# Two-tile sums one per product, the last row splits six steps earlier, and band matrices in four parts

## The chip, the cores and the metric

The program runs on one core of one Trainium2 chip. Its engines are TensorE (PE, with its weight loads as PEld), VectorE (DVE), ScalarE (ACT), GpSimd (POOL) and SyncE (SP); each takes its own queue of instructions in order, and they meet at semaphores. The metric is the device time of one execution in microseconds, less is better. The times are medians of runs; one further execution was recorded by the hardware profiler, and all rows below are from it.

## The reference, cut to what matters

Two layers of a streaming encoder run over 512 prompt rows and 32 sample rows (T = 544 columns in the kernel's layout, feature dimension on the partitions). Layer 0 mixes by stick-breaking attention and a gated linear recurrence, layer 1 by trailing means over windows of 2, 4, 8 and 16 rows. After either mixer comes the same kind of feed-forward block:

```
def swiglu(x, w_gate, w_up, w_down):
    return (jax.nn.silu(x @ w_gate) * (x @ w_up)) @ w_down
x = x + swiglu(rmsnorm(x, norm_ffn[layer]), ffn_gate[layer], ffn_up[layer], ffn_down[layer])
```

D_MODEL is 1024, D_FF is 2816, all of it float32. The pooling of layer 1 is, for each of four groups of 256 channels, the mean over the last `win` rows less the row itself, then a 256x256 map and a scale; the result is added to x. At the end there is one more RMS norm.

## The kernel before

**Precision.** A float32 operand is split into a high part in the fp32r form (ACT copy, line 822) and the low rest (DVE subtraction, line 823), and a product is made of three matmuls: high by high, high by low, low by high. One such split of a weight tile of 128x1024 is what `Supply.split` issues.

**Feed-forward block.** The 22 tiles of 128 hidden features are worked in 11 pairs, `fp` = 0 to 10. The gate and up products of a pair use a seven-product scheme on 2x2 blocks (`strassen`): 7 forms, each for gate and for up, so 14 products `n` = 0 to 13 of 12 matmuls (line 925). The forms of a pair are a11, t1, t2, t3, a12, a22 and t4; t1 and t3 are sums of two weight blocks, and are made by a second DMA that POOL issues with accumulation (line 836) after SP has loaded the first block (line 838); t2 and t4 are added on DVE (line 845).

**Down product.** The product with `ffn_down` is done in groups of hidden tiles, spread over later pairs: `due(fp)` gives the tiles and the half of the 1024 output features that pair `fp` works on. Pairs 1 and 2 work on the group of tiles 0 and 1 (two tiles), pairs 3 to 10 on groups of four, and the last group (18, 19, 21, 20) comes after all pairs: in `last_down` in layer 0, in `final` in layer 1. Each such pair has 8 sums (4 output tiles by 2 halves of the columns); a sum is 3 matmuls per hidden tile into one of the two PSUM banks of the tag `sm` (line 997), then a DVE addition to x (line 1000) that frees the bank. The loop over the products says after which product how many sums are issued: none before product 5, three after it, one after each of 6 to 10.

**Supply.** The order of loads, splits and additions of weights on SP, POOL, ACT and DVE is written out by a planner, the class `Supply`. Every operation has a due step; the clock `beat` ticks once for each product and each sum, and `ahead` issues what has come due, in order, if enough of 17 buffers (`slot`, `give`) are free. If a product needs a weight that has not been split yet, `need` issues the operations up to it at once. `pair` and `rows` hold the due steps. A `ffn_down` row block is a load (SP, line 802) and a split. For the last group the four blocks, in the order (tiles 18 and 19, half 0), (20 and 21, half 0), (18 and 19, half 1), (20 and 21, half 1), have their due steps in one line, counted from step 234, at which the products of the 11 pairs are over:

```
self.rows(PAIRS, ((-9, -5), (-8, -3), (-3, 3), (-1, 5)))
```

The first number of each is the load, the second the split. Layer 1 has a `Supply` of its own; its first loads (t1 and a11 of pair 0) are written after the block of layer 0 and take the next free buffers of the same list.

**Order of the queues.** In the feed-forward blocks PE, DVE, ACT and SP keep the written order. POOL is not in that list: a scheduler orders it. Between the layers (pooling) only PE keeps the written order. So an ACT or DVE instruction that is written in the pooling stage can be queued between instructions of the feed-forward block ahead of it.

**Bands.** The pooling of layer 1 uses banded matrices, `bf`, `bm` and `bl`, that POOL builds from memsets, `affine_select` and subtractions. `bands` is called in `ffn` of layer 0 through the table `mid`, in the written order just ahead of product 4 of pair 1. Their first use is after layer 0, in `pool_out`.

Of the kernel before, what the change touches and what calls it, by code (L numbers as in the profile page):

```python
# [9 lines left out]
F32 = mybir.dt.float32  # L10
# [4 lines left out]
P = 128  # L15
# [12 lines left out]
WINDOWS = (2, 4, 8, 16)  # L28
# [3 lines left out]
def kernel(  # L32
# [8 lines left out]
    ve, ac, gp, pe = nc.vector, nc.scalar, nc.gpsimd, nc.tensor  # L41

    cst = ctx.enter_context(tc.tile_pool(name="cst", bufs=1))
    big = ctx.enter_context(tc.tile_pool(name="big", bufs=1))
# [26 lines left out]
    def small(t="sm"):  # L71
        return psm.tile([P, 512], F32, tag=t, name=nm(t))
# [18 lines left out]
    def phase(table):  # L91
        ins = ac.preload_act_table_set(table).ins
        for p in phases[1]:
            tc.add_manual_dep(ins, p.name, nosync, reason="table")
        phases[0], phases[1] = [ins], []
# [111 lines left out]
    class Norm:  # L207
        def __init__(self, gcol):
            self.gcol = gcol
            self.xh, self.xl = [], []  # L210
            self.acc = s2.tile([P, T + NS], F32, tag="nacc", name=nm("nacc"), bufs=1)[:, :T]
# [468 lines left out]
    n1 = []  # L680
# [65 lines left out]
    PAIRS = DFF // P // 2  # L746
# [26 lines left out]
    class Supply:  # L773
# [4 lines left out]
        def __init__(self, l):  # L778
            self.l, self.raw, self.w, self.start = l, {}, {}, None
            self.ops = []  # L780
            for fp in range(PAIRS):
                self.base = 22 * fp - 8 * bool(fp)
                self.pair(fp)
            self.base += 22
            self.rows(PAIRS, ((-9, -5), (-8, -3), (-3, 3), (-1, 5)))
            self.ops.sort(key=lambda o: o[0])

        def due(self, fp):
# [94 lines left out]
    supply = Supply(0)  # L883
# [15 lines left out]
    def one(n):  # L899
        return pone.tile([P, 512], F32, tag="one", name=nm(n))  # L900
# [80 lines left out]
    def ffn(sup, nin, after=None, mid={}, last=None, first=None):  # L981
        hid = {} if first is None else first

        def down(fp):

            fs, hs = sup.due(fp)

            def bank(m, hf, s):
                beat.tick(sup)
                while any(f not in hid for f in fs):  # L990
                    beat.tick(sup)
                c = slice(P * (m % 4), P * (m % 4 + 1))
                ps = small()[:, :HN]
                for i, f in enumerate(fs):
                    (wh, wl), (a, b) = sup.row(f, m // 4), hid[f]
                    for j, (lt, r) in enumerate(((wh, a), (wh, b), (wl, a))):
                        pe.matmul(ps, lhsT=lt[:, c], rhs=r[:, s], start=i == 0 and j == 0,  # L997
                                  stop=i == len(fs) - 1 and j == 2)
                xs = x[:, m, s]
                ve.tensor_add(xs, xs, ps)  # L1000
                if hf and m % 4 == 3:
                    for f in fs[::2]:
                        sup.done((f // 2, m // 4))

            return [lambda a=(m, hf, s): bank(*a) for h in hs for m in range(4 * h, 4 * h + 4) for hf, s in HALVES] if fs else []

        def last_down():


            fs, _ = sup.due(PAIRS)  # L1010
            groups = [(0, 1)] + [(m,) for m in range(2, KD)]
            for ms in groups:
                ps = {(m, h): one("ps")[:, :HN] for m in ms for h in range(2)}
                for i, f in enumerate(fs):
                    for (m, h), o in ps.items():
                        (wh, wl), (a, b) = sup.row(f, m // 4), hid[f]
                        c, s = slice(P * (m % 4), P * (m % 4 + 1)), HALVES[h][1]
                        for j, (lt, r) in enumerate(((wh, a), (wh, b), (wl, a))):
                            pe.matmul(o, lhsT=lt[:, c], rhs=r[:, s], start=i == 0 and j == 0,  # L1019
                                      stop=i == len(fs) - 1 and j == 2, skip_group_check=True)  # L1020
                    if i % 2 or len(ms) > 1:
                        beat.tick(sup)
                for (m, h), o in ps.items():
                    xs = x[:, m, HALVES[h][1]]
                    ve.tensor_add(xs, xs, o)
                for m in ms:
                    beat.later(1, lambda m=m: after(m))
            beat.flush()
            for h in range(2):
                for f in fs[::2]:  # L1030
                    sup.done((f // 2, h))

        for fp in range(PAIRS):
            if fp or first is None:
                prods, sums = strassen(sup, nin, fp, hid), down(fp)
                for n, f in enumerate(prods):
                    if (fp, n) in mid:
                        mid[fp, n]()
                    f()
                    for _ in range(0 if n < 5 else 3 if n == 5 else 1):  # L1040
                        if sums:
                            sums.pop(0)()
        if last:
            last()
        beat.flush()
        if after:
            last_down()
        return hid
# [5 lines left out]
    BW = HN - NS - P  # L1054
    NL = 512 - P - 3 * BW
# [5 lines left out]
    def band(o, win, off):  # L1061

        n = o.shape[1]
        gp.affine_select(o, o, pattern=[[1, n]], compare_op=ALU.is_ge, fill=0.0, base=off, channel_multiplier=-1)
        gp.affine_select(o, o, pattern=[[-1, n]], compare_op=ALU.is_ge, fill=0.0, base=win - 1 - off, channel_multiplier=1)

    def bands():
        eye = big.tile([P, P], F32, name="eye")[:, :BW]
        gp.memset(eye, 1.0)
        band(eye, 1, 15)  # L1070
        eyl = cst.tile([P, NL], F32, name="eyl")[: NL + 15]
        gp.memset(eyl, 1.0)
        band(eyl, 1, 15)
        for g, win in enumerate(WINDOWS):
            gp.memset(bf[:, g], 1.0 / win)
            gp.memset(bm[:, g], 1.0 / win)
            for c in range(win - 1):
                gp.memset(bf[:, g, c : c + 1], 1.0 / (c + 1))
            band(bf[:, g], win, 0)
            band(bm[:, g], win, 15)  # L1080
            gp.tensor_sub(bf[:, g], bf[:, g], ident)
            gp.tensor_sub(bm[:, g], bm[:, g], eye)
            sa = bl[0:NS, g, NL:]
            gp.memset(sa, 1.0 / win)
            band(sa, win, 0)
            gp.tensor_sub(sa, sa, ident[:NS, :NS])
            ha = bl[32:47, g, NL:]
            gp.memset(ha, 1.0 / win)
            band(ha, win, 15)
            la = bl[: NL + 15, g, :NL]  # L1090
            gp.memset(la, 1.0 / win)
            band(la, win, 15)
            gp.tensor_sub(la, la, eyl)
# [16 lines left out]
    def pool_hist(i):  # L1110
        pw, hraw = pool["w"], pool["hraw"]
        if not i:
            ph = small()
            pe.transpose(ph[:, :120], hraw[:120, :P], ident[:120, :120])
            ve.tensor_copy(hist, ph[:, :120].rearrange("p (t k) -> p k t", k=KD))
            ptb.append(slot("pts"))
        phh = small()
        for k in range(4 * i, 4 * i + 4):
            pe.matmul(phh[32:47, 256 * (k // 2 % 2) : 256 * (k // 2 % 2 + 1)], lhsT=hist[:, k],
                      rhs=pw[k // 2][:, 256 * (k % 2) : 256 * (k % 2 + 1)], start=k % 2 == 0, stop=k % 2 == 1)  # L1120
        ac.activation(ptb[0][32:47, 512 * i : 512 * (i + 1)], phh[32:47], AF.Copy)
# [18 lines left out]
    def scales(n):  # L1140
        n.out = n.rs()
        phase("silu_and_others")
# [1 line left out]
    ET = mybir.EngineType  # L1144
    queues = {ET.PE, ET.DVE, ET.Activation, ET.SP}
    with tc.manual_schedule(engines=queues):
        ffn(supply, n1[0], after0, {(0, 3): lambda: scales(n1[0]), (0, 7): lambda: n1[0].out(), (1, 4): bands,
                                    (PAIRS - 1, 7): pool_load}, lambda: [pool_hist(i) for i in range(2)])


# [12 lines left out]
    supply = Supply(1)  # L1163
# [152 lines left out]
    with tc.manual_schedule(engines=queues):  # L1316
        final(supply, ffn(supply, n3, first=first))
# [37 lines left out]
```

## Time and profile before

| what | value |
|---|---|
| runs | 1100.87, 1104.32, 1105.19 us; median 1104.32 |
| profiled execution | 1103.79 us |
| its span, first to last instruction | 1102.0 us |
| mean granted TensorE clock | 0.98 |
| busy: PE, PEld, DVE, ACT, POOL | 95%, 91%, 70%, 45%, 19% of the span |
| chain that ended last, by engine | PE 75%, DVE 10%, issue 6%, ACT 5%, DMA 2%, POOL 1% |
| feed-forward of layer 0, of layer 1 (products and sums) | 267.5 to 655 us, 688 to 1060 us |

The span runs from the first to the last instruction; the profiled execution's time is 1.8 us longer. "Busy" is the share of the span in which an engine works. The chain is the work that ended last, followed back from the end: at each step to what released an instruction, or to the instruction ahead of it on its engine. PE is busy nearly all the time, so what counts is where PE waits, and for whom.

### The profile page before, as it was taken

What the parts mean: (1) busy time and instruction counts of PE and PEld (TensorE: products, weight loads), DVE (VectorE), ACT (ScalarE), POOL (GpSimd) and SP (SyncE); (2) the same over time, 40 slices, a digit from 0 to 9 for tenths busy, and PEclk for the clock granted to TensorE, in tenths of its full rate; (3) what the DMA queues carried; (4) which work ended last, traced back from release to release, by engine and by line L of the source; (5) the groups of instructions that cost most, each with busy time, mean ns of one, the idle gap of its engine ahead of it and who ended that gap; (6) DMA issues with size and microseconds to landing.
All of it is one profiled execution on the core that took longest, in us unless ns stands there. A gap on an engine that the chain in (4) does not pass through costs nothing.

```text
span 1102.0 us, 19760 instructions
## 1 busy us (share of the span) xinstructions
PE 1044.4 (95%) x7971; PEld 1002.9 (91%) x7971; DVE 768.4 (70%) x1236; ACT 491.7 (45%) x825; POOL 210.7 (19%) x331
## 2 busy tenths in 40 slices
PE   8979999999899999999999989599999999999987
PEld 7978888899899999999999878499999999999976
DVE  6776666767777777767776575957777766677643
ACT  7555555544643344332444354644434434334422
POOL 5162225103421101111110211111011111010100
PEclk8989999999999999999999998889999999999999
DMA  8412222414877467756566532256655676656602
GB/s 221 140 50 68 68 58 90 106 52 106 158 158 144 106 120 168 173 135 132 125 127 153 128 88 34 62 116 148 139 116 122 146 172 149 135 122 125 167 33 81
DMA packets 210955, 130.63 MB, mean 119 GB/s; under 512 B 7224, under 2 KB 195872, under 8 KB 210865
## 3 DMA queue, kind: packets, MB, share of 16 engines
q1 hardware_dynamic: 162528, 103.11, 33.2%
q0 software_dynamic: 47696, 25.16, 17.6%
q8 instruction: 62, 1.02, 0.4%
q10 hardware_dynamic: 640, 1.12, 0.3%
q14 instruction: 29, 0.23, 0.1%
HBM read 124.76 MB, written 4.60 MB: 117 GB/s over the span
## 4 chain that ended last, share of the span: by engine, by line
PE 75%; DVE 10%; issue 6%; ACT 5%; DMA 2%; POOL 1%; SPq 0%; ACTq 0%; DVEq 0%; POOLq 0%
PE xy L925 30%; PE sm L997 17%; PE z L925 11%; PE acc L168 10%; ACT ha L822 2%; DVE la L823 2%; DVE sB L474 1%; DMA raw<-in_hyb_w_in_dram 1%; PE ps L1019 1%; PE pa L1173 1%; POOL sA L493 1%; ACT y L1294 1%; DVE y L1300 1%; DMA rt<-in_ffn_up_dram 1%; DVE lt L823 1%
## 5 line engine op out<-in xcount | busy, mean ns | idle before, releaser
L997 PE MATMUL sm<-hh,h 128*128 128x272 f32 x576 | 168.0, 292 | 7.0 <-DVE x L1000 6.2
L836 POOL DMA_DIRECT2D rt<-in_ffn_gate_dram x44 | 57.0, 1295 | 589.4 <-DMA rt<-in_ffn_gate_dram 382.3
L997 PE MATMUL sm<-hl,h 128*128 128x272 f32 x576 | 165.6, 287 | 0.0
L997 PE MATMUL sm<-hh,l 128*128 128x272 f32 x576 | 165.4, 287 | 0.0
L823 DVE TENSOR_TENSOR lt<-rt,ht 128x1024 fp32r<-128x1024 f32 x88 | 107.9, 1226 | 50.7 <-ACT ht L822 50.6
L997 PEld LDWEIGHTS sm<-hh,h 128*128 128x128 f32 x576 | 108.4, 188 | 11.3 <-DVE x L1000 11.3
L98 ACT ACTIVATE s<-s 128x544 f32<-128x544 f32 x44 | 29.0, 659 | 187.1 <-DVE s L934 182.4
L997 PEld LDWEIGHTS sm<-hh,l 128*128 128x128 f32 x576 | 108.4, 188 | 0.0
L997 PEld LDWEIGHTS sm<-hl,h 128*128 128x128 f32 x576 | 108.4, 188 | 0.0
L925 PE MATMUL xy<-b,ha 128*128 128x272 f32 x704 | 103.6, 289 | 0.8 <-DVE x L678 0.8
L823 DVE TENSOR_TENSOR la<-ra,ha 128x1024 fp32r<-128x1024 f32 x66 | 81.0, 1227 | 29.1 <-ACT ha L822 29.1
L822 ACT ACTIVATE ht<-rt 128x1024 fp32r<-128x1024 f32 x88 | 92.5, 1051 | 11.5 <-DVE rt L845 6.1
L925 PEld LDWEIGHTS xy<-b,ha 128*128 128x128 f32 x704 | 93.9, 188 | 1.3 <-DVE x L678 1.0
L1000 DVE TENSOR_TENSOR x<-x,sm 128x272 f32<-128x272 f32 x160 | 69.2, 432 | 31.8 <-PE sm L997 30.8
L168 PE MATMUL acc<-xh,whi 128*128 128x272 f32 x320 | 75.4, 317 | 2.5 <-ACT xh L98 2.5
L836 POOL DMA_DIRECT2D rt<-in_ffn_up_dram x44 | 76.5, 1739 | 2.0 <-DMA rt<-in_ffn_up_dram 1.5
L976 ACT ACTIVATE hh<-u 128x544 fp32r<-128x544 f32 x44 | 29.0, 659 | 97.5 <-DVE u L965 49.9
L822 ACT ACTIVATE ha<-ra 128x1024 fp32r<-128x1024 f32 x66 | 67.3, 1051 | 6.1 <-DMA ra<-in_ffn_up_dram 4.9
L168 PE MATMUL acc<-xl,whi 128*128 128x272 f32 x320 | 68.2, 294 | 0.5 <-DVE xl L228 0.5
L168 PE MATMUL acc<-xh,wlo 128*128 128x272 f32 x320 | 67.9, 293 | 0.0
L925 PE MATMUL xy<-n,ht 128*128 128x272 f32 x352 | 54.1, 295 | 11.4 <-DVE n L293 6.9
L943 ACT ACTIVATE c<-xy 128x272 f32<-128x272 f32 x44 | 17.5, 398 | 95.2 <-PE xy L925 95.2
(381 smaller groups left out, 2525.1 us busy)
## 6 DMA issues: line engine op xcount, KB each, us to landing
r<-in_ffn_down_dram SPq DMA_DIRECT2D x44, 512.0 KB, 6.0
ra<-in_ffn_gate_dram SPq DMA_DIRECT2D x66, 256.0 KB, 5.3
ra<-in_ffn_up_dram SPq DMA_DIRECT2D x66, 256.0 KB, 6.8
rt<-in_ffn_gate_dram SPq DMA_DIRECT2D x44, 256.0 KB, 3.3
rt<-in_ffn_up_dram SPq DMA_DIRECT2D x44, 256.0 KB, 4.5
rt<-in_ffn_gate_dram POOLq DMA_DIRECT2D x44, 256.0 KB, 6.0
rt<-in_ffn_up_dram POOLq DMA_DIRECT2D x44, 256.0 KB, 7.1
raw<-in_hyb_w_in_dram SPq DMA_DIRECT2D x20, 512.0 KB, 3.9
```

Source lines behind the costliest of these rows:

```text
L98: i = ac.activation(*a, **k).ins
L168: pe.matmul(ps[:, h, : s.stop - s.start], lhsT=a[:, wi, :], rhs=b[:, s], start=first and j == 0, stop=last and j == 2)
L474: ve.tensor_tensor_scan(r, r, r, 1.0, op0=ALU.mult, op1=ALU.min)
L493: gp.affine_select(t[:, N - P :], t[:, N - P :], pattern=[[-1, P]], compare_op=ALU.is_gt, fill=fill, base=0, channel_multiplier=1)
L822: ac.activation(hi, raw, AF.Copy)
L823: ve.tensor_tensor(lo, raw, hi.bitcast(F32), op=ALU.subtract)
L836: gp.dma_start(v(t)[:, u], w, accum_op=ALU.add)
L925: pe.matmul(o, lhsT=lt, rhs=r, start=first and n == 0, stop=n == 11, skip_group_check=True)
L943: ac.activation(pc, o, AF.Copy)
L976: beat.later(n, lambda: ac.activation(a, t, AF.Copy))
L997: pe.matmul(ps, lhsT=lt[:, c], rhs=r[:, s], start=i == 0 and j == 0, stop=i == len(fs) - 1 and j == 2)
L1000: ve.tensor_add(xs, xs, ps)
```

## The change

It has three parts.

- **Sums.** In a pair whose group has fewer than four tiles (pairs 1 and 2 of either layer), one sum is issued after each product from product 4 on, until the 8 are done (after product 11). Before, three came after product 5 and one after each of 6 to 10. Pairs with four-tile groups keep their order.
- **Row splits.** The loads and splits of the four row blocks of the last group get due steps 219, 220, 222, 223 (loads) and 225, 226, 228, 230 (splits); before they were 225, 226, 231, 233 and 229, 231, 237, 239. This holds for both layers.
- **Bands.** `bands` is called four times, for one window each, ahead of product 4 of pairs 2, 4, 6 and 8 of layer 0, in place of once ahead of product 4 of pair 1. The two helper tiles `eye` and `eyl` are declared outside of it, and filled in the first call.

```
-            self.rows(PAIRS, ((-9, -5), (-8, -3), (-3, 3), (-1, 5)))
+            self.rows(PAIRS, ((-15, -9), (-14, -8), (-12, -6), (-11, -4)))
...
                     f()
-                    for _ in range(0 if n < 5 else 3 if n == 5 else 1):
+                    few = len(sup.due(fp)[0]) < 4
+                    for _ in range(n > 3 if few else 0 if n < 5 else 3 if n == 5 else 1):
                         if sums:
                             sums.pop(0)()
...
-    def bands():
-        eye = big.tile([P, P], F32, name="eye")[:, :BW]
-        gp.memset(eye, 1.0)
-        band(eye, 1, 15)
-        eyl = cst.tile([P, NL], F32, name="eyl")[: NL + 15]
-        gp.memset(eyl, 1.0)
-        band(eyl, 1, 15)
-        for g, win in enumerate(WINDOWS):
+    eye = big.tile([P, P], F32, name="eye")[:, :BW]
+    eyl = cst.tile([P, NL], F32, name="eyl")[: NL + 15]
+
+    def bands(*gs):
+        if 0 in gs:
+            gp.memset(eye, 1.0)
+            band(eye, 1, 15)
+            gp.memset(eyl, 1.0)
+            band(eyl, 1, 15)
+        for g in gs:
+            win = WINDOWS[g]
...
-        ffn(supply, n1[0], after0, {(0, 3): lambda: scales(n1[0]), (0, 7): lambda: n1[0].out(), (1, 4): bands,
+        ffn(supply, n1[0], after0, {(0, 3): lambda: scales(n1[0]), (0, 7): lambda: n1[0].out(), **{(2 * g + 2, 4): lambda g=g: bands(g) for g in range(4)},
                                     (PAIRS - 1, 7): pool_load}, lambda: [pool_hist(i) for i in range(2)])
```

## Rows read from the trace of the kernel before

**Rows 1.** Windows, layer 0: pair 1, pair 3; span, then busy time of each engine.
```profile
296.54:325.44 28.90, 27.36 (x218) 27.14 (x217) 22.55 (x35) 12.60 (x19) 5.19 (x4) 1.00 0.85 173
...
354.49:387.89 33.40, 33.37 (x266) 33.15 (x266) 23.93 (x36) 13.34 (x20) 5.19 (x4) 1.00 0.61 136
```

**Rows 2.** Waits of PE, whole span: us in total, times, longest.
```profile
PE sm L997 <- DVE x L1000: 6.2, 4, 1.6
...
PE sm L243 <- DVE nacc L219: 4.5, 1, 4.5
...
PE ps L1019 <- DVE x L1025: 2.9, 2, 2.1
PE sm L1285 <- ACT h L822: 2.7, 1, 2.7
...
PE xy L925 <- ACT b L941: 2.1, 1, 2.1
...
PE xy L925 <- ACT a L939: 1.1, 1, 1.1
...
PE sm L1285 <- DVE l L823: 0.6, 1, 0.6
```

**Rows 3.** Timeline of PE in pair 1, layer 0: start, us, instruction, idle before.
```profile
304.06 1.17 PE L925 MATMUL xy<-n,ht 128*128 128x272 f32 x8
...
306.94 0.29 PE L997 MATMUL sm<-hh,l 128*128 128x272 f32 x1
308.77 0.39 PE L997 MATMUL sm<-hh,h 128*128 128x272 f32 x1 [1.54 <-DVE x L1000]
```

**Rows 4.** Timeline of DVE in the same pair.
```profile
303.00 1.22 DVE L823 TENSOR_TENSOR l<-r,h 128x1024 fp32r<-128x1024 f32 x1
...
307.15 1.22 DVE L823 TENSOR_TENSOR la<-ra,ha 128x1024 fp32r<-128x1024 f32 x1 [1.79 <-ACT ha L822]
308.29 0.43 DVE L1000 TENSOR_TENSOR x<-x,sm 128x272 f32<-128x272 f32 x1
```

**Rows 5.** Timeline of ACT from the last product to the end.
```profile
1063.29 1.28 ACT L92 ACT_TABLE_LOAD   x1
1064.58 2.00 ACT L822 ACTIVATE h<-r 128x1024 fp32r<-128x1024 f32 x2
1079.63 0.59 ACT L1294 ACTIVATE y<-sm 32x512 f32<-32x512 f32 x1 [13.04 <-PE sm L1285]
```

**Rows 6.** Timelines of SP, ACT, DVE and PE at the end of layer 0.
```profile
621.76 0.37 SPq L838 DMA_DIRECT2D rt<-in_ffn_gate_dram  x1
...
630.39 0.37 SPq L838 DMA_DIRECT2D ra<-in_ffn_gate_dram  x1
...
635.00 1.06 ACT L822 ACTIVATE ha<-ra 128x1024 fp32r<-128x1024 f32 x1 [4.94 <-DMA ra<-in_ffn_up_dram]
635.96 0.73 ACT L227 ACTIVATE xs<-x,cols 128x544 fp32r<-128x544 f32 x1
...
631.97 1.56 DVE L1025 TENSOR_TENSOR x<-x,ps 128x272 f32<-128x272 f32 x4 [0.47 <-PE ps L1019]
...
639.95 1.22 DVE L823 TENSOR_TENSOR la<-ra,ha 128x1024 fp32r<-128x1024 f32 x1
...
663.19 0.98 PE L243 MATMUL sm<-ones,nacc 128*128 128x1 f32 x4 [4.48 <-DVE nacc L219]
```

**Rows 7.** Window behind that wait; the number after POOL's is the granted clock.
```profile
663.20:668.00 4.80, 4.80 (x25) 4.75 (x26) 2.13 (x8) 2.31 (x6) 0.86 (x2) 0.50 0.93 117
```

**Rows 8.** POOL: one form of line 1064, and its timeline.
```profile
L1064 POOL TENSOR_SCALAR_AFFINE_SELECT eye<-eye x1: 516/516/516, 15.3 to 15.3; 128x112 f32<-128x112 f32 x1
...
214.74 0.61 POOL L1104 DMA_DIRECT2D hraw<-in_state_pool_dram  x1 [5.03 <-issue]
266.80 0.21 POOL L1075 MEMSET bf<- 128x128 f32 x1 [51.45 <-PE acc L168]
...
271.09 1.30 POOL L836 DMA_DIRECT2D rt<-in_ffn_gate_dram  x1
```

## The prediction

> **What bounds the kernel now.** I read the share of busy time first: PE works 95% of the span, so only time in which PE waits, or runs at the lower clock, can be won. The table by stage shows where. A pair with four-tile sums is full: 33.37 of 33.40 us [rows 1]. Pair 1, with two-tile sums, is not: 27.36 of 28.90 us. It issues 14 x 12 + 8 x 6 = 216 matmuls; at 27.36 us / 218 = 0.1255 us each, these want 27.11 us, so 1.79 us are lost. The list of PE's waits names the place: four waits of up to 1.6 us on the addition of line 1000, 6.2 us in all [rows 2], one for each two-tile group in either layer. In the timeline, the second sum's last matmul starts at 306.94 and the third sum's first at 308.77 [rows 3]: 1.83 us where 0.13 us would do. DVE shows why: the first sum's bank is freed by an addition that starts at 308.29, queued behind a weight split begun at 307.15, which had itself waited for ACT [rows 4]. Three short sums in a row want a third bank where there are two.
>
> The same list has two more places that the change touches: the end of the program (line 1285, 2.7 + 0.6 us) and the passage from layer 0 to the pooling (lines 1019 and 243, 2.9 + 4.5 us) [rows 2].
>
> **Part 1, the sums.** Matmuls, evictions, loads and splits keep their number; only their order moves. Now a product lies between two sums, so a bank is wanted again after product, sum, product: 1.51 + 0.75 + 1.51 = 3.8 us (12, 6 and 12 matmuls of 0.1255 us). Ahead of the eviction DVE has at most the split of one form and one addition, 1.22 us each by [rows 4], 2.4 us. So the wait goes and nothing takes its place. The first sum comes a product earlier, at 304.06 [rows 3]; its row weights' low part is ready at 303.00 + 1.22 = 304.22 [rows 4], and is used by the third matmul, at 304.31: just in time. Per group the gain lies between the wait (6.2 / 4 = 1.55 us) and the whole gap (1.83 us); I take 1.75 us, near the 1.79 us by counting, since a restarted PE also loses a little behind the wait. Four groups: **7.0 us**, bounds 6.2 and 7.3.
>
> **Part 2 at the end of layer 1.** I followed the planner's list step by step, with its 17 buffers. Before, the blocks of half 1 are due at steps 237 and 239, but the products end at 234, so `final` has to force both splits through `need`. They then stand on ACT behind the table load at 1063.29 and start at 1064.58 [rows 5]; PE waits 2.7 us for the high and 0.6 us for the low part [rows 2]. With the new steps all four splits lie in pair 10, and no operation finds too few buffers. Both waits go: 3.3 us, and the restart with them; I take **3.4 us**, bounds 2.7 (the low part still late) and 3.6. All of it reaches the end, because the output stage starts on ACT when PE lets it, after 13.04 us idle [rows 5], and its tail hangs on that.
>
> What the splits meet in pair 10: two more of them there, 2 x 1.22 us on DVE and 2 x 1.0 us on ACT (two take 2.00 us [rows 5]). DVE has 9.5 us idle in such a pair, ACT 20 [rows 1], so I cost this at nothing; without that cover it would be 2.4 us a layer. On SP the four row loads move up past nothing but each other; behind them on that queue are only the first loads of the next layer, and behind those, on POOL, their accumulating loads, which can only come earlier.
>
> **Part 2 at the end of layer 0.** Here the half 1 blocks are not late for PE. But layer 1's first loads take over their buffers. Before, the t1 load of layer 1 goes into a buffer that product 13 frees (issued at 621.76), and the a11 load into the raw buffer of a row block, free only once that block's late split is done (630.39) [rows 6]. Now t1 gets a buffer that product 11 frees, and a11 one that product 13 frees: it starts some 8.6 us earlier. Before, ACT meets the split of a11 with its data still on the way and stands 4.94 us, until 635.00, with the norm's copies of line 227 queued behind; the first of these runs at 635.96 [rows 6]. It could have run when the first two of the four additions that start at 631.97 were over, at about 632.75: 3.2 us late. From there DVE and ACT hand each other the work tile by tile to the norm, for which PE waits 4.5 us at 663.19 [rows 2, 6], so a shift of this chain arrives. Three more DVE instructions for layer 1, of 1.2 us each, the first at 639.95 [rows 6], stand inside this chain; with the loads earlier some can go in front of it. I take 3.2 + 1.2 = **4.4 us**; the bounds are 0 (other early splits stand in ACT's way the same) and 3.2 + 3.6 = 6.8. I choose above the middle because a11's wait has a plain cause that is taken away.
>
> After the wait at 663.19, PE runs 4.8 us at a granted clock of 0.50, the lower level of 1.2 GHz [rows 7]. If PE stood less before that, the clock could stay up and those 4.8 us fall to 2.4. The Trainium skill (TensorE: Matmul & The Clock Gate, "HAM oscillation — how this bites in real kernels") says that idle gaps throttle the engine and that it then starts cold; the row agrees, and by that rule the sum would hold up to 2.4 us more. I leave it out of the sum: a shift of 4.4 us mostly moves both ends of this wait.
>
> **Part 3, the bands.** Where the call is written does not place the work: POOL isn't among the queues in written order. `eye`, written in pair 1, is cut at 15.3 us; the load of line 1104, written in pair 10, runs at 214.74; and the first memset of `bf` sits at POOL's head from then to 266.80, until the mixer's last matmuls free its memory [rows 8]. All of that is earlier than the old or the new call, and the four calls' instructions are free to run at the same moment. So I expect the bands where they are, and **0 us**. Bounds: if they did leave, the accumulating load at 271.09 [rows 8] would no longer wait for them, and PE's waits on the copies of lines 939 and 941 in pair 0, 1.1 + 2.1 us [rows 2], could go: 3.2 us. A loss from bands in later pairs has the same size at most, for POOL's pair is otherwise 5.2 of 33 us busy [rows 1].
>
> **Sum.** 1103.79 - 7.0 - 3.4 - 4.4 = 1088.99, so **1089.0 us**. The profiled execution is 0.5 us under the median of the runs, 1104.32, which I neglect.
>
> **The rivals.**
> - *The passage gives nothing.* The scheduler puts another split of layer 1 in front of the norm's copies, and ACT waits for that. For it: the ACT order there comes from a schedule, not from the text, and the old order already misjudged a load. Against: the load comes 8.6 us earlier. 1103.79 - 10.4 = 1093.4 us.
> - *The bands leave as well.* 1089.0 - 3.2 = 1085.8 us. Against it stand the rows of POOL.
> - *The clock stays up.* 1089.0 - 2.4 = 1086.6 us.
> - *The first sum waits instead of the third.* The low row weights come just in time in pair 1 [rows 3, 4]; if every group waits 1.75 us at its first sum, part 1 nets nothing: 1103.79 - 7.8 = 1096.0 us.
> - *DVE becomes the bound in the two-tile pairs, and the kernel slower.* DVE keeps its 22.55 us [rows 1] in a pair that shrinks to 27.1 us, 83%. If evictions came late at each of the 32 sums, it would decide: slower by over 0.5% needs 1103.79 + 5.5, so the 7.8 us of part 2 and 5.5 more have to be lost, 13.3 us over 32 sums, 0.42 us at each, say 1112 us at 0.5. Against it: a bank is free for 3.8 us, and it takes four instructions of 1.22 us in front of an eviction to use that up; the planner puts two there.
> - *The change doesn't do what it says*, of part 3 alone, is in the forecast.
>
> **How the numbers follow.** Chances: the forecast 0.60, the passage gives nothing 0.18, bands 0.07, clock 0.06, first sum 0.05, slower 0.04. A change of 0.5%, 5.5 us, is about what a measurement of this kernel can tell from none: the bound for faster is 1098.8 us. The first five lie below it; for their sizes being smaller together than their bounds, and for runs that spread over 4 us, I take 0.08 of them as no change. Faster 0.88, same 0.08, slower 0.04. Range: the lower end has all upper bounds, 7.3 + 3.6 + 6.8 and the clock's 2.4, 20.1 us: 1084. The upper end has the lower bounds, 6.2 + 2.7 + 0, 8.9 us: 1094.9, and half the spread of the runs, 2.2 us: 1097.
>
> **What would show it.** Right: no wait of line 997 above 0.5 us, pairs 1 and 2 at 27.1 us in both layers; no wait of line 1285 on line 822, and no split behind the table load at the end; the a11 load issued together with that of t1, line 227 first at 1 us after the additions, the wait before line 243 over some 4 us earlier in its stage; bands in one piece behind the mixer's end. Wrong: a wait of line 997 on the row weights, an ACT wait on a load of layer 1 in front of line 227, or band work at the later pairs.

## The result, and the profile after

The changed kernel takes **1089.18 us** (median; 1087.01 to 1090.10) where the kernel before took 1104.51 us beside it: a ratio of 0.9866, 95% interval 0.9844 to 0.9888, or 14.8 us (12.4 to 17.2). Predicted were 1089.0 us. Its profiled execution has a span of 1087.7 us, 14.3 us less. In the changed file the lines behind the loop over the products have moved down by one, those behind `bands` by four.

Where the 14.3 us lie, as differences between the starts of PE's instructions in the two timelines:

| stretch | before, us | after, us | difference |
|---|---|---|---|
| start to the first product of layer 0 | 267.50 | 266.78 | -0.72 |
| pair 0, layer 0 | 29.04 | 29.03 | 0 |
| pairs 1 and 2, layer 0 | 57.79 | 54.23 | -3.56 |
| pairs 3 to 10, layer 0 | 267.24 | 267.25 | 0 |
| history (its transposition to the first sum of the last group) | 5.21 | 7.87 | **+2.66** |
| last group and the wait, to line 243 | 36.41 | 32.53 | **-3.88** |
| line 243 to the first product of layer 1 | 25.08 | 25.59 | +0.51 |
| pair 0, layer 1 | 46.43 | 44.00 | **-2.43** |
| pairs 1 and 2, layer 1 | 57.86 | 54.19 | -3.67 |
| pairs 3 to 10 of layer 1 and the output, to the last matmul | 303.00 | 299.79 | -3.21 |

So part 1 gave 7.2 us, the end of layer 1 gave 3.2, and the passage between the layers 3.1 (2.66 - 3.88 + 0.51 - 2.43). The 0.7 us at the start are no effect of the change: over the profiles of this study that start lies anywhere from 265.1 to 267.8 us. The stretch from line 243 to the first product of layer 1 takes 24.9 to 26.4 us in the twelve profiles in which its first wait is left as it is, so its 0.51 us say little either.

The windows of after, against [rows 1, 7]. Columns: span, busy time of PE, PEld, DVE, ACT and POOL, granted clock, DMA share, GB/s. The stretches are pair 1, pair 3, the history's products and the work behind line 243:

```profile
295.81:322.97 27.16, 27.16 (x219) 27.14 (x217) 22.83 (x36) 12.74 (x19) 5.19 (x4) 1.00 0.89 183
350.04:383.44 33.40, 33.35 (x266) 33.13 (x265) 23.65 (x36) 13.33 (x20) 5.19 (x4) 1.00 0.56 123
619.91:625.16 5.25, 5.25 (x17) 1.88 (x17) 1.22 (x2) 1.65 (x2) 0.83 (x1) 0.67 0.87 105
657.70:662.50 4.80, 4.80 (x28) 4.75 (x29) 2.15 (x8) 2.88 (x7) 1.22 (x3) 0.56 1.06 132
```

Pair 1 is as full as pair 3 now. The third line is new: the history's products ran at a granted clock of 0.67, where they had 1.00 before. The same stretch before:

```profile
623.23:626.78 3.55, 3.55 (x16) 1.45 (x16) 1.21 (x2) 0.59 (x1) 1.53 (x2) 1.00 0.46 136
```

The list of PE's waits, against [rows 2]:

```profile
PE sm L243 <- DVE nacc L219: 4.0, 1, 4.0
...
PE sm L1123 <- DVE hist L1119: 2.4, 1, 2.4
...
PE sm L1289 <- DVE hl L973: 0.4, 1, 0.4
```

The waits of line 997, of line 1019 and of line 1285 on the splits (6.2, 2.9 and 3.3 us) are gone; the wait for the copy of the history was 1.4 us and is 2.4.

Timelines of PE and DVE in pair 1, against [rows 3, 4]: start, length, instruction.

```profile
303.34 0.29 PE L997 MATMUL sm<-hh,h 128*128 128x272 f32 x1
...
303.59 0.36 PE L997 MATMUL sm<-hh,l 128*128 128x272 f32 x1
...
304.16 1.17 PE L925 MATMUL xy<-n,ht 128*128 128x272 f32 x8
...
305.66 0.29 PE L997 MATMUL sm<-hh,h 128*128 128x272 f32 x1
...
303.42 1.22 DVE L823 TENSOR_TENSOR lt<-rt,ht 128x1024 fp32r<-128x1024 f32 x1
304.56 0.43 DVE L1000 TENSOR_TENSOR x<-x,sm 128x272 f32<-128x272 f32 x1
```

The first sum's bank is freed at 304.99, and the third sum doesn't want it before 307.92. The third matmul, the first to use the row weights' low part, shows 0.36 us in place of 0.29: that is all that is left of the rival in which the first sum waits.

The end of layer 0, against [rows 6]: SP, ACT, DVE, PE.

```profile
614.46 0.37 SPq L838 DMA_DIRECT2D rt<-in_ffn_gate_dram  x1
...
616.98 0.37 SPq L838 DMA_DIRECT2D ra<-in_ffn_gate_dram  x1
...
612.87 1.04 ACT L822 ACTIVATE h<-r 128x1024 fp32r<-128x1024 f32 x1
...
620.78 1.06 ACT L822 ACTIVATE ha<-ra 128x1024 fp32r<-128x1024 f32 x1 [0.92 <-DMA ra<-in_ffn_up_dram]
...
631.21 0.75 ACT L227 ACTIVATE xs<-x,cols 128x544 fp32r<-128x544 f32 x1 [4.67 <-DVE x L1025]
...
613.94 1.23 DVE L823 TENSOR_TENSOR l<-r,h 128x1024 fp32r<-128x1024 f32 x1 [1.68 <-ACT h L822]
615.09 0.43 DVE L1000 TENSOR_TENSOR x<-x,sm 128x272 f32<-128x272 f32 x1
...
619.59 0.27 DVE L1119 COPY hist<-sm 128x120 f32<-128x120 f32 x1
...
630.36 1.56 DVE L1025 TENSOR_TENSOR x<-x,ps 128x272 f32<-128x272 f32 x4 [3.06 <-PE ps L1019]
...
657.69 1.76 PE L243 MATMUL sm<-ones,nacc 128*128 128x1 f32 x12 [4.00 <-DVE nacc L219]
```

The a11 load now follows the t1 load by 2.5 us, ACT stands 0.92 us for its data and not 4.94, and line 227 starts 0.85 us behind the start of the additions. New is the line at 613.94: the last of the four row splits stands on DVE for 1.68 us, waiting for ACT, with the addition of line 1000 and the chain to the copy of the history queued behind it.

The end of layer 1 on ACT, against [rows 5], has no split behind the table load; POOL, against [rows 8], has the bands where they were, from the first memset of `bf` to the last subtraction, behind the mixer and in one piece:

```profile
1053.07 1.28 ACT L92 ACT_TABLE_LOAD   x1
1065.40 0.59 ACT L1298 ACTIVATE y<-sm 32x512 f32<-32x512 f32 x1 [11.04 <-PE sm L1289]
...
266.08 0.21 POOL L1079 MEMSET bf<- 128x128 f32 x1 [50.95 <-PE acc L168]
...
285.00 1.44 POOL L1085 TENSOR_TENSOR bf<-bf,ident 128x128 f32<-128x128 f32 x1
```

### The profile page after: what moved, and what is told of

The parts are those of the page before. It is cut to its first block, busy times and chain, and to the rows that moved or that the text cites. A ratio compares the mean times of both kernels' runs of the same rounds, so it can differ in the third digit from the quotient of the medians.

```text
span 1087.7 us, 19757 instructions
## 1 busy us (share of the span) xinstructions
PE 1043.3 (96%) x7971; PEld 1002.0 (92%) x7971; DVE 767.3 (71%) x1236; ACT 492.2 (45%) x825; POOL 210.8 (19%) x331
## 4 chain that ended last, share of the span: by engine, by line
PE 77%; DVE 10%; issue 5%; ACT 3%; DMA 2%; POOL 2%; SPq 0%; ACTq 0%; DVEq 0%; POOLq 0%
PE xy L925 30%; PE sm L997 18%; PE z L925 11%; PE acc L168 10%; PE ps L1019 2%; DVE sB L474 1%; DVE la L823 1%; DMA rt<-in_ffn_up_dram 1%; DMA raw<-in_hyb_w_in_dram 1%; PE pa L1177 1%; ACT ha L822 1%; POOL sA L493 1%; PE pb L1177 1%; DVE y L1304 1%; ACT y L1298 1%
## 5 line engine op out<-in xcount | busy, mean ns | idle before, releaser
L823 DVE TENSOR_TENSOR la<-ra,ha 128x1024 fp32r<-128x1024 f32 x66 | 80.9, 1226 | 24.9 <-ACT ha L822 24.2
L925 PE MATMUL xy<-n,ht 128*128 128x272 f32 x352 | 54.4, 296 | 10.2 <-DVE n L293 7.2
L168 PEld LDWEIGHTS acc<-xh,whi 128*128 128x128 f32 x320 | 50.4, 193 | 9.8 <-issue 5.7
```

What stands on the lines that cost most here:

```text
L168: pe.matmul(ps[:, h, : s.stop - s.start], lhsT=a[:, wi, :], rhs=b[:, s], start=first and j == 0, stop=last and j == 2)
L823: ve.tensor_tensor(lo, raw, hi.bitcast(F32), op=ALU.subtract)
L925: pe.matmul(o, lhsT=lt, rhs=r, start=first and n == 0, stop=n == 11, skip_group_check=True)
```

## The experiments

Ratios are against the kernel before on the same chip; its medians there were 1103.51, 1102.24 and 1104.75 us for the three sets of four.

**Each part alone: the sums.**

```
+                    few = len(sup.due(fp)[0]) < 4
+                    for _ in range(n > 3 if few else 0 if n < 5 else 3 if n == 5 else 1):
```

> The kernel before with part 1 alone (two-tile sums one per product). Theory (a third short sum in a row waits for a bank that DVE frees late): in the two profiled executions pairs 1 and 2 went from 28.9 to 27.1 us in both layers, 7.2 us in all, so 1104.5 - 7.2 = 1097.3 us; no wait of line 997 on line 1000 in the list of waits, and the ends of both layers as before (waits of line 1019 2.9 us, of line 1285 2.7 us). Rival (the sums now wait on their row weights, or the gain is given back at the end of the layer): under 4 us, 1100.5 us or more, with a wait of line 997 on line 822 or 823, or longer waits at lines 1019 and 243.

1097.48 us, ratio 0.994 (0.9923 to 0.9958): 6.6 us (4.6 to 8.5). The four short pairs take 27.17, 27.07, 27.07 and 27.11 us, no wait of line 997 is listed, and the waits at both ends stay. The theory holds. One line of its windows was not expected, in the output stage behind the 2.7 us wait:

```profile
1059.00:1066.00 7.00, 7.00 (x28) 5.03 (x27) 0.51 (x1) 0.00 (x0) 0.00 (x0) 0.70 0.01 2
```

The granted clock is 0.70 behind the wait on the late split; in the profile of before it stayed at 1.00 behind the same wait:

```profile
1065.69:1072.69 7.00, 6.39 (x31) 4.46 (x32) 2.34 (x2) 0.90 (x1) 0.00 (x0) 1.00 0.01 2
```

From pair 3 of layer 1 to the last matmul this kernel needs 305.17 us, before 303.00.

**The row splits alone, in both layers.**

```
-            self.rows(PAIRS, ((-9, -5), (-8, -3), (-3, 3), (-1, 5)))
+            self.rows(PAIRS, ((-15, -9), (-14, -8), (-12, -6), (-11, -4)))
```

> The kernel before with part 2 alone (row loads and splits of the last group six steps earlier in both layers). Theory from the two traces: 3.1 us at the end of layer 0 and 3.1 us at the end of layer 1, 6.2 us, so 1098.3 us, with the four waits of line 997 on line 1000 still there (6.2 us). The prediction's sizes, 4.4 + 3.4 = 7.8 us, would give 1096.7 us. Rival (the passage from layer 0 to the pooling gives nothing of itself): 3.1 us, 1101.4 us.

1097.25 us, ratio 0.9931 (0.9905 to 0.9958): 7.6 us (4.6 to 10.5). The interval holds both sizes, 6.2 and 7.8, and not the rival's 3.1. Its history waits 2.3 us as in the changed kernel, but the clock did not fall behind it:

```profile
623.19:626.74 3.55, 3.55 (x16) 1.45 (x16) 1.22 (x2) 1.64 (x2) 0.85 (x1) 1.00 1.15 144
```

From the history's transposition to the first sum of the last group it takes 6.16 us: 0.95 more than before, all of it the wait.

**The bands alone**, the diff's third part on the kernel before.

> The kernel before with part 3 alone (the band matrices called in four parts in pairs 2, 4, 6 and 8). Theory (POOL takes no notice of where the call is written): no change, 1104.5 us within 0.2%, with the first memset of bf still at 266 us and the last band instruction at about 285 us. Rival (the bands do move): the accumulating load at 271.09 us comes earlier and PE's waits of line 925 on the copies of lines 939 and 941 (1.1 + 2.1 us) go, down to 1101.3 us; or up to 3.2 us more if later pairs' accumulating loads come late.

1102.54 us, ratio 0.9989 (0.9971 to 1.0007): nothing that can be told from no change. The first memset of `bf` starts at 266.15 us, the accumulating load at 270.44. The theory holds.

**The row splits in layer 0 alone, and in layer 1 alone** (the new steps with `if l == 0`, or `if l == 1`, else the old ones).

> The kernel before with part 2 in layer 0 alone. Theory from the traces: the additions and the norm's copies come earlier (3.4 us less between the first sum of the last group and the last, 0.5 us less before line 243), 2.7 us are lost ahead of them, because the extra split in pair 10 delays the copy of the history (wait of the history's products 2.4 us in place of 1.4) and PE's clock then falls (history's products 5.2 us in place of 3.6), and the clock's return in pair 0 of layer 1 decides over 2.4 us: 0.7 us faster without it, 3.1 us with it, so 1101.4 to 1103.8 us. The prediction's step, a shift of 4.4 us that arrives whole: 1100.1 us. Rival (nothing): 1104.5 us.

1100.16 us, ratio 0.9971 (0.9954 to 0.9988): 3.2 us (1.3 to 5.1). From the first sum of the last group to line 243 it takes 32.52 us against 36.41 before, the history 7.85 us against 5.21, and its products 5.24 us, as in the changed kernel. Nothing gained is excluded; the interval holds the first theory's 3.1 and the prediction's 4.4, but not that theory's lower end, 0.7.

> The kernel before with part 2 in layer 1 alone. Theory: the two waits of line 1285 on the late splits (2.7 + 0.2 to 0.6 us) go, which gives 3.2 us, and PE's clock, which fell behind that wait in three of four profiles that have it (0.70 to 0.77 of full speed over some 9 us, 2.2 us lost) and not in the profile of before, stays up: 3.2 to 5.4 us, 1098.1 to 1100.3 us against 1103.5 us. The prediction's size: 3.4 us, 1100.1 us. Rival (the extra splits in pair 10 cost as much as they save): over 1102 us, with waits of PE in pair 10 of layer 1.

1099.65 us, ratio 0.9979 (0.9967 to 0.999): 2.3 us (1.1 to 3.6). From pair 3 to the last matmul its profile has 299.85 us against 303.00, 3.2 us less, and neither wait is left. The 5.4 us are excluded. This suggests that over the runs of the kernel before the clock's fall costs little of its 2.2 us, though three other profiles with that wait (sums, bands and layer 0 alone, 305.1 to 305.3 us) show it whole; only one profile of each kernel is there to see it.

**What delays the history.** The changed kernel with the last row split of layer 0 due at step 231, not 230; on DVE, up to the copy of the history, this only puts the split behind two instructions that stood behind it. On ACT the split of a11 now stands behind the history's two copies from PSUM; both kernels run it after the copy of line 1119.

```
+            self.rows(PAIRS, ((-15, -9), (-14, -8), (-12, -6), (-11, -4 if l else -3)))
```

> The changed kernel with the last of the four row splits of layer 0 due one step later (231 in place of 230), which puts its DVE subtraction behind the addition of line 1000 and the product of line 936, and the split of a11 behind the two copies of the history. Theory (that split delays DVE's chain to the copy of the history by 1.0 us): the wait of PE for the history goes from 2.4 us back to 1.4 us, the history's products take 3.6 us as before, everything behind stays: 1 to 2.7 us faster than the changed kernel's 1089.2 us, 1086.5 to 1088.2 us. Rival (the copy is late because the additions and products of the last products came later, not for the split): the wait stays 2.4 us, 1089.2 us.

The profile shows the theory's mechanism: the copy of the history follows the last product by 1.0 us less, the wait is 1.4 us again, and the products take 3.55 us at a granted clock of 1.00. Its timeline of DVE, and its window of the history's products:

```profile
613.00 0.44 DVE L1000 TENSOR_TENSOR x<-x,sm 128x272 f32<-128x272 f32 x1 [0.70 <-PE sm L997]
613.35 0.72 DVE L936 TENSOR_TENSOR s<-s,rs 128x544 f32<-128x544 f32 x1
613.99 1.22 DVE L823 TENSOR_TENSOR l<-r,h 128x1024 fp32r<-128x1024 f32 x1
...
618.65 0.28 DVE L1119 COPY hist<-sm 128x120 f32<-128x120 f32 x1
```
```profile
618.98:622.53 3.55, 3.55 (x16) 1.45 (x16) 1.21 (x2) 0.59 (x1) 1.82 (x2) 1.00 1.04 178
```

The time, 1087.23 us at 0.9869 (0.9854 to 0.9884), can't be told from the changed kernel's 0.9866. Of the 2.7 us won at the history the profile shows 2.6 lost again in pair 0 of layer 1, which takes 46.58 us here and 44.00 there.

**The history's transposition earlier.**

```
+    def pool_turn():
+        ph = small()
+        pe.transpose(ph[:, :120], pool["hraw"][:120, :P], ident[:120, :120])
+        ve.tensor_copy(hist, ph[:, :120].rearrange("p (t k) -> p k t", k=KD))
...
+    (PAIRS - 1, 12): pool_turn
```

> The changed kernel with the transposition of the history and its copy to SBUF written ahead of product 12 of pair 10 in layer 0 instead of behind product 13. Theory (PE waits there for nothing but this copy): the wait of 2.4 us goes, and the clock that fell behind it in two of three profiles with a wait of 2.3 to 2.4 us stays up (1.7 us): 2.4 to 4.1 us faster than the changed kernel's 1089.2 us, 1085.1 to 1086.8 us, unless the clock takes up to 2.4 us back in pair 0 of layer 1. Rival (the passage is bound by the chain of DVE and ACT and not by PE): the wait before line 243 grows by as much, 1089.2 us.

From pair 10 to the first sum of the last group it needs 37.17 us, the changed kernel 41.28: 4.1 us less, the upper end. The history's products follow the last product at once and take 3.62 us. The wait before line 243 stays (4.1 us), so the rival falls. The time is 1086.43 us, 0.9863 (0.9842 to 0.9883), which can't be told from the changed kernel's; pair 0 of layer 1 again is a long one, 46.72 us, and gives 2.7 us back.

**The bands really moved.**

```
-            gp.memset(bf[:, g], 1.0 / win)
-            gp.memset(bm[:, g], 1.0 / win)
+            ve.memset(bf[:, g], 1.0 / win)
+            ve.memset(bm[:, g], 1.0 / win)
```

> The changed kernel with the two full-size memsets of each window's bf and bm done by DVE, which keeps the written order, so that POOL's band work for bf and bm is really done in pairs 2, 4, 6 and 8 (eight memsets change engine, some 0.2 us each on DVE). Theory (the prediction's bound): the accumulating load at 270.38 us in the trace of the changed kernel no longer stands behind band work and starts by up to 4 us earlier; PE's waits of line 925 on lines 939 and 941 in pair 0 of layer 0 (1.1 + 2.1 us) shrink or go: 0 to 3.2 us faster than 1089.2 us, 1086.0 to 1089.2 us. Rival A (those waits hang on ACT's own queue, with two table loads of 1.28 us in it, and not on the load): 1089.2 us. Rival B (the band work then delays the accumulating loads of pairs 3, 5, 7 and 9): up to 3.2 us slower, with waits of PE on DMA or on line 822 there.

Pair 0 of layer 0 takes 26.27 us in place of 29.03. Its timelines of POOL and PE; its window of pair 0; the same window of the changed kernel:

```profile
252.01 1.28 POOL L836 DMA_DIRECT2D rt<-in_ffn_gate_dram  x1 [38.69 <-DVE tmp L314]
...
278.21 1.27 PE L925 MATMUL xy<-t,ht 128*128 128x272 f32 x8 [2.31 <-ACT b L941]
```
```profile
265.08:291.35 26.27, 23.84 (x184) 23.04 (x184) 20.04 (x32) 16.22 (x28) 2.59 (x2) 1.00 0.47 124
```
```profile
266.78:295.81 29.03, 25.61 (x183) 24.37 (x184) 22.56 (x33) 16.71 (x29) 22.27 (x60) 0.94 0.76 155
```

The band work is now in the later pairs (its first instruction at 326.15 us, in pair 2). The accumulating load starts 18 us earlier, not 4 (16.7 us counted from the first product of layer 0): a memset at POOL's head that waited for the mixer's memory had held it, and then 4.3 us of band work. The wait of line 925 on line 939 (1.1 us) is gone; the one on line 941 is not (2.31 us), so there rival A is right. The rest of the 2.8 us is the clock, 1.00 in place of 0.94 over the pair (29.03 x 0.06 = 1.7 us), and it isn't shown to come from the bands. In two kernels whose bands stayed the clock did not fall in this pair either (the row splits alone 28.08 us, in layer 1 alone 27.57), and in one with the bands moved, the last kernel of this section, it fell (27.73). Compared at the same clock, the bands moved are worth 0.9 to 1.8 us in this pair. Pair 1 gives back 0.6 us, 0.4 of it a wait of line 997 on the low row weights. Pairs 3 to 10 give back another 0.55, with one wait of 0.6 us on an addition of line 1000; no wait there is on a load or on line 822, as rival B would have it. The time is 1085.53 us, 0.9858 (0.9838 to 0.9877); the 1.6 us that the profile has less over pairs 0 to 10 can't be told from the changed kernel's 0.9866.

**Another order of the short sums:** two after product 5, then one after each of 6 to 11.

> The kernel before with another order of the two-tile sums: two after product 5 (before: three), then one after each of products 6 to 11. Theory (two banks, so a third short sum in a row is what waits): no wait of line 997 on line 1000, pairs 1 and 2 at 27.1 us, the same gain as with one sum per product from product 4 on: 7 us, 1096 to 1097.5 us against 1103 us. Rival (DVE needs a product between any two short sums): a wait is left behind product 6, and the gain is 3 to 5 us, 1098 to 1100 us.

1093.3 us, ratio 0.9908 (0.9887 to 0.9929): 10.2 us (7.8 to 12.5), more than either theory. No wait of line 997 is listed, and the short pairs take 27.38 to 27.42 us, so the third sum in a row was what waited; in pair 1 some 0.3 us stay, since the third sum, with one product ahead of it, still starts as the first sum's addition ends (307.60 us). The sums give 6.1 of the 11.9 us that this profile is shorter than before's. Of the surplus, 2.5 us are the short pair 0 of layer 1, 1.2 lie ahead of pair 1 of layer 0, and 2.0 are in the passage, where the order on ACT, which a scheduler sets, came out another way, as ACT's timeline shows:

```profile
628.58 0.75 ACT L227 ACTIVATE xs<-x,cols 128x544 fp32r<-128x544 f32 x1 [2.77 <-DVE x L1025]
...
629.79 0.73 ACT L227 ACTIVATE xs<-x,cols 128x544 fp32r<-128x544 f32 x1
...
630.98 1.04 ACT L822 ACTIVATE ha<-ra 128x1024 fp32r<-128x1024 f32 x1
```

The a11 load is issued late as before (626.15 us), but its split stands behind the norm's copies here, and line 227 starts 0.85 us behind the additions (627.73 us) as in the changed kernel. From the first sum of the last group to the last it takes 26.03 us; with the sums alone it was 29.54. So this kernel has much of part 2's gain in layer 0 without part 2, by a reordering that its edit did not aim at.

**The clock behind line 243.** The changed kernel with work that nobody uses put into the wait:

```
+                wm = one("wm")
+                for _ in range(30):
+                    pe.matmul(wm[:, :256], lhsT=n2.xh[0][:, :P], rhs=pwh[:, :256], start=True, stop=True)
```

> The changed kernel with 30 more matmuls of 256 columns, whose result is not used, in the wait of 4.0 us before line 243 (30 x 0.118 = 3.5 us). Theory (the granted clock of 0.50 to 0.56 behind that wait is what PE's standing costs): the clock stays at 1.00 there, PE's work from 657.69 to 666.4 us (8.7 us, of which 3.2 us are the clock's) takes 5.5 us, and the layer 1 block starts 3.2 us earlier: 1086.0 us against 1089.2 us. Rival (behind line 243 the chain of ACT and DVE sets the pace, not PE): the clock stays up and the block starts at most 1 us earlier, 1088.2 to 1089.2 us.

Its timeline of PE, and a window behind the wait:

```profile
654.48 3.75 PE L1224 MATMUL wm<-pwh,xs 128*128 128x256 f32 x30
658.72 1.38 PE L243 MATMUL sm<-ones,nacc 128*128 128x1 f32 x12 [0.49 <-DVE nacc L219]
```
```profile
662.00:666.00 4.00, 4.00 (x37) 3.89 (x35) 0.74 (x1) 2.70 (x5) 0.00 (x0) 1.00 0.11 16
```

The clock stays at 1.00, and line 243 to the first product of layer 1 takes 22.65 us in place of 25.59: 2.9 us, so PE sets the pace there and the rival falls. The time is 1087.13 us, 0.985 (0.9828 to 0.9872); by the runs this can't be told from the changed kernel's 0.9866.

**Together:** the transposition and the bands, and then the filling matmuls as well.

> The changed kernel with both the history's transposition ahead of product 12 and the memsets of bf and bm on DVE. The two are in different stages; theory: their gains in the profiles add up, 4.1 us in the passage and 2.2 us in pairs 0 to 10 of layer 0, 6.3 us, 1082.9 us against 1089.2 us, and by up to 2.6 us more or less as the clock stands in pair 0 of layer 1. Rival (both only shift the phase of the clock, and runs spread by as much): 1085.5 to 1087 us, as either alone.

1086.02 us, 0.9837 (0.9815 to 0.986). From the first product of layer 0 to that of layer 1 the profile has 410.20 us, the changed kernel's 416.50: 6.3 us, just the sum, with the clock at 1.00 in pair 0 of layer 0 again. Pair 0 of layer 1 takes 46.69 us and gives 2.7 back. The time lies in the rival's range and not at the theory's 1082.9, and can't be told from the changed kernel's: the runs don't show the sum that the profile shows.

> The same with the 30 filling matmuls as well. Theory (what PE's standing before line 243 costs in clock is 3.2 us and reaches the end): 1079.7 us. Rival (ACT and DVE set the pace behind line 243): as without the filling matmuls, 1082 to 1083 us.

1082.27 us, ratio 0.9807 (0.9784 to 0.983): 21.3 us under the kernel before, and the interval lies wholly under the changed kernel's. Line 243 to the first product takes 22.56 us, 2.9 less than without the filling (25.43), as the theory has it. The time is 3.8 us under that of the kernel without the filling, but the two intervals overlap, and in the profiles 2.6 us of the difference are pair 0 of layer 1, which is a short one here (44.07 us). That the time itself is the rival's 1082 and not 1079.7 comes from the base, which was 1086.0 and not 1082.9 us.

## Why the prediction was right, and where it was not

**Part 1, 7.0 us: right in mechanism and size.** 7.2 us in the profile, 6.6 alone. The place, the third sum's bank, is shown from two sides: one sum per product and two in a row both take the wait away.

**End of layer 1, 3.4 us: right.** 3.2 us in the profile, 2.3 (1.1 to 3.6) alone. What the working did not have is the clock: behind the same 2.7 us wait it fell in three of the five profiles that have it, 2.2 us each.

**End of layer 0, 4.4 us: the mechanism right, the arrival wrong.** The load comes 2.5 us behind t1's, ACT stands 0.9 us for it and not 4.9, line 227 starts when predicted, and from the first sum of the last group to line 243 there are 3.88 us less: 3.1 for line 227 (predicted 3.2) and 0.7 in the chain behind it (1.2 taken). In all nine profiled kernels with the new steps in layer 0 line 227 follows the additions by 0.85 us; with the old ones it is 3.6 to 4.0 us in four kernels, and 0.85 in the one with the other order of the short sums. That one shows the cause once more: with the split of a11 behind line 227, the stall goes though the load is late.

But ahead of it 2.66 us were lost, and the step that failed is the one that reads "DVE has 9.5 us idle in such a pair, ACT 20 [rows 1], so I cost this at nothing". Idle time of a whole pair says nothing on one place in a written order: the last split waits 1.68 us on DVE for ACT, and the chain to the history's copy stands behind it. Moved by one step, the split costs nothing (shown). It costs 1.0 us as a wait and, in three of five profiles with that wait, 1.7 us as clock. So the change gives 3.88 - 2.66 = 1.2 us here where the clock falls, and 3.88 - 0.95 = 2.9 where it doesn't. The rival in which the passage gives nothing falls all the same: twelve runs of layer 0 alone give 3.2 us (1.3 to 5.1).

**The clock.** That the wait before line 243 would keep its low clock was right (0.56). In pair 0 of layer 1 the profile after is 2.43 us shorter. No run shows this to be the change's: over all profiles that pair takes 43.8 to 44.1 us in eight kernels and 46.3 to 46.8 us in six, with the old row steps and the new in either group. The difference lies behind the last of five waits of PE in that pair. That wait ends 26.3 us after the pair's start in all fourteen profiles, and then the same matmuls run without a wait, before and after:

```profile
714.53:734.70 20.17, 20.17 (x128) 19.93 (x129) 9.24 (x21) 6.90 (x14) 2.69 (x2) 0.78 0.49 106
```
```profile
709.54:727.28 17.74, 17.74 (x128) 17.50 (x129) 9.08 (x21) 6.90 (x14) 0.00 (x0) 0.90 0.52 116
```

So it is PE's clock alone, 0.90 in place of 0.78 over this stretch; in the eight short pairs it is 0.90 to 0.92, in the six long ones 0.77 to 0.78. Why it stays low for longer in some stays open; a kernel that fills PE's waits in that pair was not tried. Without these 2.43 us the passage would have given 0.7 us (1.2 less the 0.51 behind line 243), and the profile 11.9.

**Part 3, 0 us: right**, and for the reason given. Its bound, 3.2 us if the bands did leave, was tried: 2.8 us in pair 0, of which only the 1.1 us of line 939 are the wait that was named, and most of the rest the clock, which isn't shown to be the bands'.

So the sum came out closer than its parts, and that is luck: of the profile's 14.3 us, 2.43 in pair 0 of layer 1 and 0.72 at the start come from no step that the change is shown to have made, and they stand in for what the passage fell short of 4.4. The parts run alone add up to 6.6 + 3.2 + 2.3 = 12.1 us, or to 14.2 with the row splits of both layers in one kernel (7.6).

## What to carry to other kernels

Where an engine keeps a written order, cost an added instruction by what stands directly behind it until its operand comes, not by the idle share of the stage. A wait of PE cost its length here and then, in three of five profiles behind 2.4 us, three of five behind 2.7 and in all behind 4.0, some three quarters as much again in clock (1.7, 2.2 and 2.9 us). Where it can't be removed, filling it with work that nobody uses is worth trying: the profile shows 2.9 us for it, the runs alone don't settle it. And what one execution shows of the clock can be chance: compare a stage over several profiles before it is put down to an edit. Last, an instruction that waits for memory at the head of a queue can hold what is queued behind it, as the memset on POOL held a load for some 17 us.

## What was not expected of the hardware

- Behind waits of one length the granted clock fell in some profiles and not in others: behind 2.3 to 2.4 us for the history to 0.67 in the changed kernel, and not at all (1.00) with the row splits alone; behind 2.7 us to 0.70 with the sums alone, and not before. Behind the 4.0 to 4.5 us before line 243 it was low in all twelve profiles without filling (0.50 to 0.57 over the next 4.8 us), and cost 2.9 us, by the experiment that filled the wait.
- The Trainium skill (TensorE: Matmul & The Clock Gate, "HAM oscillation — how this bites in real kernels") describes idle gaps after which PE starts cold. The rows agree [rows 7], and filling the wait took the cold start away. The prediction put the low clock behind line 243 at up to 2.4 us, half of the 4.8 us in [rows 7]; the experiment gives 2.9.
- POOL's accumulating load stood behind a memset of 0.2 us that waited 50.95 us for memory, and came some 17 us later for it, counted from the first product of layer 0 (270.38 us with the memset at the head, 252.01 without).
